# Fewer and wider attention matmuls, index scores between projections, and larger expert pieces in a two-block network kernel

## The chip, the cores and the metric

The kernel runs on one core of one Trainium2 chip. The metric is the device time of one execution in microseconds (us). The engines are PE (matrix products; PEld is its loading of weights), DVE, ACT and POOL (element-wise work) and SP (which issues DMAs here). Line numbers such as L1195 are those of the kernel before; in the changed kernel the same code stands a few to some fifty lines lower or higher.

## What is computed

Two network blocks run one after the other on 512 tokens of width 1024, all in fp32. The first block is a Hyena convolution and a differential attention (16 heads over 528 positions: the 512 tokens and 16 meta positions). The second has a sparse attention (DSA, 8 heads), a block attention (NSA, 8 heads) and a mixture of 32 experts. The parts that the change touches, cut from the reference:

```python
def attend(qb):                                   # differential attention, T = 528 keys
    s = jnp.einsum("bqhmd,bkhmd->bhmqk", qb, k) * scale
    p = jax.nn.softmax(s, axis=-1)
    p = p[:, :, 0] - lam * p[:, :, 1]
    return jnp.einsum("bhqk,bkhd->bqhd", p, v)

# DSA: index scores choose the keys (8 index heads of 32 columns)
idx_logit = jax.nn.relu(jnp.einsum('bthd,bsd->bths', qi, ki))
score = jnp.einsum('bth,bths->bts', wi, idx_logit)
_, sel = lax.top_k(where(causal, score, -inf), k_sel)
# ... softmax over the chosen keys, then p @ v with heads of 64 columns

# NSA: three branches per head (compressed, selected, window), 64 columns each
o = gc * o_cmp + gs * o_slc + gw * o_win

# MoE: two of 32 experts per token
gate, up = jnp.split(xb @ w_gate_up[e], 2, axis=-1)
y = (jax.nn.silu(gate) * up) @ w_down[e]
```

## The kernel before

The tokens stand in tiles of 128. A product that must be exact to fp32 is made of three matmuls of a number split in a high and a low part (`split`, L326 on ACT and L327 on DVE: `hi = cast(x)`, `lo = x - hi`): hi·hi, lo·hi and hi·lo. Where a plain fp32 operand is used (the experts), one matmul in the program is two records in the trace. A scheduler orders each engine's instructions from the order of the code, its priorities and the tiles that are free; generators that `yield` are merged by `interleave`, so that projections fill the time in which attention waits for its softmax.

*Differential attention* (about 830 to 1395 us) runs over eight groups of two heads. `v_proj` (L1195 to L1197) makes the values with the tokens as stationary operand, in five token tiles of 128, 128, 128, 128 and 16 rows (`TT`); the last one takes 3 x 8 matmuls for 16 rows. `S` (L1269, L1270) makes the scores, L1271 and L1272 the negative maximum and its scaling on DVE, L1274 the exponential. For each of the five key tiles the probabilities are transposed (L1291, into `pt`), split into `pth` and `ptl`, and multiplied with the values (L1296 `vh·pth`, L1297 `vh·ptl`, L1298 `vl·pth`); the fifth tile has 16 keys and takes three matmuls of its own per head.

*Projections and index scores of the second block* (about 1545 to 1697 us). The code makes the compressed keys, the queries and keys, the transposes of the compressed probabilities (`ptc`, L1570), then the index queries `qi`, and after all of that the index scores: for three token tiles `i` (256, 384 and 512 keys) and 8 heads, three matmuls of 32 rows each (L1585 to L1587) into one of two `pi` tiles, a ReLU on ACT (L1589) and a weighted sum on DVE (L1591, L1593).

*NSA and DSA attention* (1697 to 2005 us). `head` makes scores for two branches of a head (L1612 to L1614), the maximum (L1617) and its scaling by -0.125 (L1618), the exponential (L1621), then for each branch and each of four key tiles transposes (L1637), a split into `pth` and `ptl`, and three matmuls (L1644, L1646, L1647) into `po`. Keys are causal, so the four take 512, 384, 256 and 128 columns. The values stand in 128 columns of which 64 are zero (`vpad`), so that the two heads of a pair add up in one `po`. The gates' projections (L808 to L812 into `pg` and `S`) fill the waits.

*Mixture of experts* (2068 to 2406 us). After the router, `prepare(g)` makes the slot matrix `P` and the indices of the tokens of four experts (`cb`, L1922). For the first group `first_gather` picks the tokens with 64 matmuls (L1957) of the normed activations `Xh`, `Xl`; from the second group on an indirect DMA (L1931, issued on POOL) picks rows of `xd` into `xg`, and `turn` transposes them (L1971) and scales them into `Xs`. `gate_up` (L1988) and `down` (L2011) then use raw fp32 weights; two experts of 64 slots work side by side, one in the columns 0 to 63 of the PE array and one in 64 to 127 (`HALF`). `combine` (L2029) puts the results back.

The weights come in one stream of 1 MB pieces on SP's queue (`WeightStream`), into a ring of raw tiles: two at first, and from the end of the router's norm three more of `N_RAW` and four of the pool of split weights (L1833, L1834).

Of the kernel before, what the change touches and what calls it, by code (L numbers as in the profile page):

```python
# [10 lines left out]
FT = mybir.dt.float32  # L11
# [9 lines left out]
D = 1024  # L21
# [21 lines left out]
def host_consts():  # L43
# [109 lines left out]
    m[:, 193:201] = pi[:, None] + 128 * np.arange(8)[None, :]  # L153
# [37 lines left out]
class WeightStream:  # L191
# [156 lines left out]
N_RAW = 3  # L348
# [9 lines left out]
def weight_jobs(A):  # L358
# [29 lines left out]
    for m in range(KD):  # L388
# [24 lines left out]
    gu = A["w_gate_up_2"][0].rearrange("e (h a p) c -> e h p a c", p=128, h=2)  # L413
    dn = A["w_down_2"][0].rearrange("e (a p) c -> e p a c", p=128)
# [11 lines left out]
def build(tc, A, C, out):  # L426
# [3 lines left out]
    with ExitStack() as ctx:  # L430
# [52 lines left out]
        with tc.tile_pool(name="xn3", bufs=1, reuse_waits="tile") as xnp:  # L483
            k.xh = xnp.tile([128, KD, T], FR, name="xh")
            k.xl = xnp.tile([128, KD, T], FR, name="xl")
            pp = ppc.enter_context(tc.tile_pool(name="b2p", bufs=1, reuse_waits="tile", space=PSUM))
            with tc.tile_pool(name="hy3", bufs=1, reuse_waits="tile") as hp:
                yh = hp.tile([128, CT, T], FR, name="yh")
                yl0 = hp.tile([128, 2, T], FR, name="yl0")
                k.hT, k.yT = (hp.tile([128, KD, T], FT, name=n) for n in ("hT", "yT"))  # L490
                nc.gpsimd.dma_start(k.hT, k.hdram)
                yl = [yl0]
                for i, raw in enumerate(k.vx.tiles):
                    if i:
                        yl.append(k.xpool.tile([128, 2, T], FR, name="vx", bufs=CT // 2))
                    for c in range(2):
                        split(k, raw[:, c, 0:SEQ], yh[:, 2 * i + c, 0:SEQ], yl[i][:, c, 0:SEQ])
                yl = Pairs(yl)
                out_norm(k, yh, yl, (slice(META, PARTS_A.stop), PARTS_B), META, 3, 4, pp,
                         (("pj", 3), ("pm", 1), ("pi", 2)))  # L500
                nc.gpsimd.dma_start(k.hdram[:, :, META:], k.hT[:, :, META:])
            k.xctx.close()
# [1708 lines left out]
```

## Time and profile before

| | before |
|---|---|
| median of 3 runs | 2430.65 us (2430.28 to 2431.44) |
| the profiled execution | 2426.15 us, of which the span is 2424.1 us |
| PE busy | 2277.2 us, 94% of the span |
| PEld busy | 78% |
| DVE, ACT, POOL busy | 65%, 44%, 29% |
| DMA, mean | 126 GB/s |

The span is what the trace covers; the rest of an execution's time lies around it. PE is busy nearly all the time, so the span is a row of stages in which PE is either at work or waits for a short chain of another engine. The tables by stretch of time below are read stage by stage. A matmul's own duration overlaps the next one's, so what a matmul costs is the distance from its start to the next start.

### The profile page before, as it was taken

The numbers are of one execution on the slowest core, as the hardware profiler recorded it, in microseconds if no ns is written. First come the engines' busy times: TensorE is split into PE (matmuls) and PEld (weight loads), VectorE is DVE, ScalarE is ACT, GpSimd is POOL, SyncE is SP. The second block draws the span as 40 slices with busy tenths as digits, with TensorE's granted clock in tenths as the row PEclk, the third lists the DMA queues.
The fourth block names the chain that finished last, engine by engine and source line by source line (L and its number), as shares of the span: only waits on it lengthen the run. The fifth ranks groups of instructions, "written<-read, shape, count | busy, mean of one in ns | idle before, by whom it ended". The sixth has DMA issues, their size and how long they took to land. (4 is left out here: it accounts for less than half of the span.)

```text
span 2424.1 us, 38020 instructions
## 1 busy us (share of the span) xinstructions
PE 2277.2 (94%) x14644; PEld 1891.3 (78%) x14644; DVE 1574.4 (65%) x3065; ACT 1075.3 (44%) x2201; POOL 709.0 (29%) x713
## 2 busy tenths in 40 slices
PE   7999999998999989999999989888999999899997
PEld 6989999997889978888888879866777777544333
DVE  7777764438985696778778744587788764434333
ACT  5666654433344464656545544434444543211111
POOL 3454541115643242233232236332011112101000
PEclk9999999999999999999999999887999999899999
DMA  6333322222136421112111136621121324698983
GB/s 223 123 118 103 119 80 88 88 86 92 57 123 187 135 76 44 53 53 70 46 52 60 54 103 177 179 70 53 53 83 53 113 77 149 249 402 329 362 322 134
DMA packets 269329, 305.19 MB, mean 126 GB/s; under 512 B 20520, under 2 KB 212404, under 8 KB 268762
## 3 DMA queue, kind: packets, MB, share of 16 engines
q1 hardware_dynamic: 228048, 245.90, 30.8%
q10 hardware_dynamic: 35834, 32.64, 4.5%
q0 software_dynamic: 5264, 24.20, 2.6%
q8 instruction: 116, 1.90, 0.3%
q14 instruction: 67, 0.55, 0.1%
HBM read 277.13 MB, written 25.58 MB: 125 GB/s over the span
## 5 line engine op out<-in xcount | busy, mean ns | idle before, releaser
L261 DVE TENSOR_TENSOR wlo<-wraw,whi 128x1024 fp32r<-128x1024 f32 (+2 forms) x201 | 229.4, 1155 | 155.6 <-ACT whi L280 136.6
L261 POOL TENSOR_TENSOR wlo<-wraw,whi 128x1024 fp32r<-128x1024 f32 (+1 forms) x91 | 181.7, 2005 | 500.0 <-ACT whi L280 321.1
L280 ACT CAST whi<-wraw 128x1024 fp32r<-128x1024 f32 x198 | 206.1, 1047 | 181.9 <-PE pj L810 57.6
L808 PE MATMUL ps<-xh,whi 128*128 128x264 f32 x1024 | 215.0, 287 | 4.8 <-ACT hTd L581 4.5
L810 PE MATMUL ps<-xl,whi 128*128 128x264 f32 x1024 | 214.6, 287 | 0.0
L812 PE MATMUL ps<-xh,wlo 128*128 128x264 f32 x1024 | 212.2, 285 | 0.0
L808 PE MATMUL pj<-xh,whi 128*128 128x512 f32 (+2 forms) x544 | 191.0, 357 | 4.3 <-DVE rr L1180 2.9
L810 PE MATMUL pj<-xl,whi 128*128 128x512 f32 (+2 forms) x544 | 188.9, 353 | 0.0
L812 PE MATMUL pj<-xh,wlo 128*128 128x512 f32 (+2 forms) x544 | 188.4, 353 | 0.1
L808 PEld LDWEIGHTS ps<-xh,whi 128*128 128x128 f32 x1024 | 161.4, 190 | 7.0 <-ACT hTd L581 5.3
L810 PEld LDWEIGHTS ps<-xl,whi 128*128 128x128 f32 x1024 | 161.7, 189 | 1.8 <-issue 1.3
L812 PEld LDWEIGHTS ps<-xh,wlo 128*128 128x128 f32 x1024 | 161.4, 190 | 1.2 <-issue 0.8
L810 PE MATMUL pj<-vx,whi 128*128 128x256 f32 (+1 forms) x480 | 135.7, 284 | 0.6 <-DVE vx L327 0.6
L326 ACT CAST pth<-pt 128x512 fp32r<-128x512 f32 (+4 forms) x174 | 84.3, 497 | 113.3 <-PE pt L1637 62.1
L327 DVE TENSOR_TENSOR ptl<-pt,pth 128x512 fp32r<-128x512 f32 (+4 forms) x174 | 98.0, 573 | 50.9 <-ACT pth L326 50.5
L1274 ACT ACTIVATE p<-S,mx 128x528 f32<-128x528 f32 x128 | 89.6, 702 | 78.7 <-DVE mx L1272 58.4
L808 PEld LDWEIGHTS pj<-xh,whi 128*128 128x128 f32 x544 | 103.3, 192 | 19.0 <-DVE rr L1180 3.3
L812 PEld LDWEIGHTS pj<-xh,wlo 128*128 128x128 f32 x544 | 102.6, 192 | 14.1 <-issue 1.0
L810 PEld LDWEIGHTS pj<-xl,whi 128*128 128x128 f32 x544 | 102.9, 192 | 13.1 <-issue 1.0
L1271 DVE TENSOR_REDUCE mx<-S 128x1 f32<-128x528 f32 x128 | 88.7, 701 | 25.7 <-PE S L1270 25.4
L1988 PE MATMUL gu<-wraw,Xs 128*64 128x512 f32 x312 | 92.5, 600 | 0.0
L810 PEld LDWEIGHTS pj<-vx,whi 128*128 128x128 f32 x480 | 90.6, 189 | 1.0 <-DVE vx L327 1.0
(677 smaller groups left out, 6716.1 us busy)
## 6 DMA issues: line engine op xcount, KB each, us to landing
wraw<-in_w_gate_up_dram SPq DMA_DIRECT2D x39, 1024.0 KB
wraw<-in_hy_w_in_dram SPq DMA_DIRECT2D x32, 1024.0 KB
wraw<-in_da_w_in_dram SPq DMA_DIRECT2D x32, 1024.0 KB
wraw<-in_hy_w_out_dram SPq DMA_DIRECT2D x16, 1024.0 KB
wraw<-in_da_w_out_dram SPq DMA_DIRECT2D x16, 1024.0 KB
wraw<-in_w_down_dram SPq DMA_DIRECT2D x16, 1024.0 KB
whi<-in_w_gate_up_dram SPq DMA_DIRECT2D x25, 512.0 KB
wlo<-in_w_gate_up_dram SPq DMA_DIRECT2D x25, 512.0 KB
```

The lines of the kernel that those rows point to most:

```text
L261: eng.tensor_tensor(l, r, h.bitcast(FT), OP.subtract)
L280: nc.scalar.copy(hf, vf)
L326: nc.scalar.copy(hi, raw)
L327: (lo_eng or nc.vector).tensor_tensor(lo, raw, hi.bitcast(FT), OP.subtract)
L808: nc.tensor.matmul(ps[i], wh[:, kk, fsl], xh[:, kk, c], start=f, stop=False)
L810: nc.tensor.matmul(ps[i], wh[:, kk, fsl], xl[:, kk, c], start=False, stop=False)
L812: nc.tensor.matmul(ps[i], wl[:, kk, fsl], xh[:, kk, c], start=False, stop=l)
L1271: nc.vector.tensor_reduce(mx[:, m:m + 1], S[:, :, 0:TH], AX.XY, OP.max)
L1274: nc.scalar.activation(p.rearrange("p (a b) -> p a b", a=2), S[:, :, 0:TH], AF.Exp, bias=mx[:, m:m + 1], scale=0.125, accum_out=sm[:, m:m ...
L1988: nc.tensor.matmul(ps[o], xs[:, kk, o], w[:, a], start=(kk == 0), stop=(kk == 7))
```

## The change

1. Differential attention. The last 16 tokens of `v_proj` now take one stationary operand `xr` of 48 columns (high part, zeros, low part), so 16 matmuls instead of 24 per group; the fifth key tile's three products are one matmul with 80 rows (L1325 after), in which high and low parts of the probabilities (`pr`) and values (`vr`) stand in rows 0 to 15, 32 to 47 and 64 to 79. The scale 0.125 goes into the queries, and the maximum is negated as it is made, so L1272 (and L1618) are gone.
2. Second block. The index queries are projected first, and the index scores (`index_scores`) are merged with the rest of the projections (`rest`), two steps for each step of `rest`.
3. NSA and DSA. `pair` works on the two heads of a pair in place of the two branches of a head. Values and probabilities stay fp32: each key tile's probabilities are copied once (DVE for the first head, ACT for the second) and multiplied by one fp32 matmul of 64 columns per head, the heads in the two halves of the array. `vpad` and its splits are gone.
4. Mixture of experts. Expert weights are laid out so that a partition's piece is 8 KB for `wraw` (four consecutive rows of a matrix) in place of four of 2 KB; the activations are stored in a permuted order to fit (`xp_`), and the hidden values are transposed with a stride of 2. The first group is gathered by indirect DMA too; `first_gather` and `Xh`, `Xl` are gone. Six raw tiles instead of three are opened, before the output projection of the second block rather than after the router's norm. `yh`, `yl` and `PT` have 3 buffers instead of 4.

The core of the diff:

```diff
@@ WeightStream.more_raw, N_RAW, weight_jobs
     def more_raw(self, *pools):
+        i = self.nr % len(self.raw_at)
+        self.raw_at = self.raw_at[i:] + self.raw_at[:i]
         self.nr = len(self.raw_at)
-N_RAW = 3
+N_RAW = 6
+    job(w, 640, 256)
     for p in range(2):
         job(w, 936 + p * 256, 256, True)
...
-    job(w, 640, 256)
-    gu = A["w_gate_up_2"][0].rearrange("e (h a p) c -> e h p a c", p=128, h=2)
-    dn = A["w_down_2"][0].rearrange("e (a p) c -> e p a c", p=128)
+    gu = A["w_gate_up_2"][0].rearrange("e (h p a) c -> e h p a c", p=128, h=2)
+    dn = A["w_down_2"][0].rearrange("e (p a) c -> e p a c", p=128)
@@ differential attention
+                if i == 4:
+                    ps = ps[:48, 0:256]
+                    for kk in range(KD):
+                        nc.tensor.matmul(ps, xr[:, kk], wh[:, kk], start=(kk == 0), stop=False)
+                        nc.tensor.matmul(ps, xr[:, kk], wl[:, kk], start=False, stop=(kk == KD - 1))
...
-                        nc.vector.tensor_reduce(mx[:, m:m + 1], S[:, :, 0:TH], AX.XY, OP.max)
-                        nc.vector.tensor_scalar(mx[:, m:m + 1], mx[:, m:m + 1], -0.125, None, op0=OP.mult)
+                        nc.vector.tensor_reduce(mx[:, m:m + 1], S[:, :, 0:TH], AX.XY, OP.max, negate=True)
...
+                    if i == 4:
+                        r = pr_
+                        nc.scalar.copy(r[0:16], pt[:16])
+                        nc.scalar.copy(r[64:80], pt[:16])
+                        nc.vector.tensor_tensor(r[32:48], pt[:16], r[0:16].bitcast(FT), OP.subtract)
+                        nc.tensor.matmul(po, vrs[h % 3][0:80], r[0:80], start=False, stop=True)
+                        continue
@@ second block: projections and index scores
+            def index_scores():
+                for i in range(1, 4):
...
+                        yield
+            def rest():
...
+            interleave((rest(), 1), (index_scores(), 2))
@@ NSA and DSA: pair in place of head
-                    split(k, pt[:, c], th[:, c], tl[:, c])
...
-                    nc.tensor.matmul(po[:, c], vh[:, kt, vc], th[:, c], start=(first and b == 0 and kt == 0), stop=False,
...
-                    nc.tensor.matmul(po[:, c], vh[:, kt, vc], tl[:, c], start=False, stop=False, skip_group_check=True)
-                    nc.tensor.matmul(po[:, c], vl[:, kt, vc], th[:, c], start=False, stop=l, skip_group_check=True)
+                    t = wk.tile([128, 512], FT, name=f"pt{m}")
+                    (nc.scalar.copy if m else nc.vector.tensor_copy)(t[:, c], pt[:, c])
+                    th.append(t)
+                for o, t in zip(HALF, th):
+                    nc.tensor.matmul(po[o, c], v[:, kt], t[:, c], start=(first and kt == 0), stop=(last and kt == 3),
@@ mixture of experts
+    rawp = ctx.enter_context(tc.tile_pool(name="moew", bufs=1, reuse_waits="tile"))
+    k.W.more_raw((rawp, N_RAW))
...
-            split(k, tp, Xh[:, :, c], Xl[:, :, c])
...
-        k.W.more_raw((rawp, N_RAW), (k.W.hl_pool, 4))
+        k.W.more_raw((k.W.hl_pool, 4))
...
-                nc.tensor.transpose(tp[:, f], x[:, f * 128:f * 128 + 128], k.ident)
+                nc.tensor.transpose(tp[:, f], x[:, 256 * (f // 2) + f % 2:256 * (f // 2) + 256:2], k.ident)
...
-            yh, yl = (yp.tile([128, 2, 512], FR, name=n, bufs=4) for n in ("yh", "yl"))
+            yh, yl = (yp.tile([128, 2, 512], FR, name=n, bufs=3) for n in ("yh", "yl"))
...
-        first_gather()
+        prepare(0)
+        for _ in turn(0):
+            pass
```

Where the order of instructions changes, on PE. The index scores before: they begin after the last transposes of `ptc` (written to `pm`), and nothing else stands between them (`pi` is their result, `kih` and `kil` the index keys, `qih` and `qil` the index queries).

```order
L810 MATMUL pj<-xl,whi 128x512
L812 MATMUL pj<-xh,wlo 128x512
L1570 MATMUL pm<-ident,blk 128x128 x4
L1585 MATMUL pi<-kih,qih_19030 128x256
L1586 MATMUL pi<-kil,qih_19030 128x256
L1585 MATMUL pi<-kih,qih_19030 128x256
L1586 MATMUL pi<-kil,qih_19030 128x256
L1587 MATMUL pi<-kih,qil_19031 128x256 x2
L1585 MATMUL pi<-kih,qih_19030 128x256
```

After, on PE, the same work (now L1561 to L1563) at the first query projections of the second block (`scp` are the compressed scores, `pj` a projection):

```order
L1586 MATMUL scp<-kcl,rl 128x32
L1561 MATMUL pi<-kih,qih_18321 128x256
L1562 MATMUL pi<-kil,qih_18321 128x256
L1563 MATMUL pi<-kih,qil_18322 128x256
L1561 MATMUL pi<-kih,qih_18321 128x256
L1562 MATMUL pi<-kil,qih_18321 128x256
L1563 MATMUL pi<-kih,qil_18322 128x256
L813 MATMUL pj<-xl,whi 128x512
L815 MATMUL pj<-xh,wlo 128x512
```

Two heads' triples now stand between projections; 16 of the 24 triples do so, and the last eight, those with 512 keys, still follow one another after the last transposes.

In the NSA attention, PE before, the products of one branch (`vsh` and `vsl` are the split values, `pt<-ident` the transposes of the next branch):

```order
L1644 MATMUL po<-pth,vsh 128x512
L1646 MATMUL po<-ptl,vsh 128x512
L1647 MATMUL po<-pth,vsl 128x512
L1644 MATMUL po<-pth,vsh 128x384
L1637 MATMUL pt<-ident,P_19576 128x128
L1637 MATMUL pt<-ident,P_19593 128x128
L1646 MATMUL po<-ptl,vsh 128x384
L1647 MATMUL po<-pth,vsl 128x384
```

After, on PE at the same place (L1678 are the products of 64 columns, `w1k` is the buffer that the values took over, L1673 the transposes, L1648 to L1650 scores):

```order
L1648 MATMUL S<-ks0h,qs 128x512
L1649 MATMUL S<-ks0l,qs 128x512
L1650 LDWEIGHTS identb
L1650 MATMUL S<-causb,identb 128x128
L1673 MATMUL pt<-ident,P_19251 128x128
L1673 MATMUL pt<-ident,P_19311 128x128
L1678 MATMUL po<-pt_19343,w1k 64x384
L1678 MATMUL po<-pt_19350,w1k 64x256
L1673 MATMUL pt<-ident,P_19311 128x128
L1678 MATMUL po<-pt_19355,w1k 64x256
L1673 MATMUL pt<-ident,P_19311 128x128
```

The two heads' products stand side by side in part only. The 96 products form 76 runs with other PE work between them: 8 pairs of 512 columns, 7 of 128, 1 of 384, 1 of 256 and 3 of 384 beside 256, and 56 alone (8 of 512, 19 of 384, 19 of 256, 10 of 128).

At the start of the experts, PE before (`cb` are token indices, `rp` the router's counts); 64 matmuls of L1957 follow up to the first `gate_up`:

```order
L1905 MATMUL pg<-ident,rk 32x128 x4
L1922 MATMUL cb<-wr,P 128x8 x8
L1957 MATMUL ga<-P,xh 128x256
L1957 MATMUL ga<-P,xl 128x256
L1957 MATMUL ga<-P,xh 128x256
```

After, on PE at the same place:

```order
L1944 MATMUL pg<-ident,rk 32x128 x4
L1961 MATMUL cb<-wr,P 128x8 x16
L2041 LDWEIGHTS sel
L2041 MATMUL cb<-rkT,sel 128x512
L1994 MATMUL gu<-ident,xg 128x128 x8
L1961 MATMUL cb<-wr,P 128x8 x8
L1994 MATMUL ga<-ident,xg 128x128 x4
L2041 LDWEIGHTS sel
L2041 MATMUL cb<-rkT,sel 128x512
L2011 MATMUL gu<-wraw,Xs 64x512 x16
```

The 64 matmuls are gone; transposes of the gathered rows `xg` stand ahead of the first `gate_up` (L2011 after).

## Rows read from the trace of the kernel before

**Rows 1.** Stretches of time: us, busy (x instructions) by engine, PEclk, DMA share, GB/s

```profile
830.00:1395.00 565.00, 541.48 (x3550) 480.75 (x3550) 438.10 (x962) 318.13 (x673) 173.87 (x194) 0.97 0.19 58
...
1575.00:1670.00 95.00, 82.44 (x442) 70.44 (x442) 77.55 (x126) 36.79 (x68) 31.71 (x30) 0.89 0.24 67
1670.00:1697.00 27.00, 20.79 (x81) 14.18 (x79) 18.98 (x32) 12.53 (x27) 3.65 (x2) 0.58 0.15 40
1697.00:2005.00 308.00, 294.01 (x1495) 230.46 (x1494) 229.92 (x557) 136.64 (x359) 43.98 (x25) 0.98 0.24 77
...
2068.00:2097.00 29.00, 20.04 (x140) 17.53 (x140) 16.91 (x72) 7.31 (x19) 1.79 (x5) 0.76 0.69 254
2097.00:2406.00 309.00, 296.13 (x1250) 121.51 (x1247) 109.34 (x194) 53.74 (x104) 24.39 (x49) 1.00 0.86 321
```

**Rows 2.** Timeline of PE, differential attention: start us, duration us, instruction, count

```profile
1027.38 0.28 PE L1195 MATMUL pj<-whi,xh 128*16 128x256 f32 x1
1027.49 0.28 PE L1196 MATMUL pj<-wlo,xh 128*16 128x256 f32 x1
...
1061.59 0.49 PE L1297 MATMUL po<-ptl,vh 16*128 16x512 f32 x1
1061.93 0.39 PE L1298 MATMUL po<-pth,vl 16*128 16x512 f32 x1
```

**Rows 3.** Groups by line, 830 to 1395: busy us, mean ns, idle before

```profile
L1272 DVE TENSOR_SCALAR mx<-mx 128x1 f32<-128x1 f32 x128 | 17.8, 145 | 0.9
```

**Rows 4.** Waits of PE from 1575 to 1697: us in total, times, longest

```profile
PE pi L1585 <- ACT qih L326: 3.2, 1, 3.2
PE pi L1585 <- ACT rl L1589: 3.0, 10, 0.7
```

**Rows 5.** Timeline of PE, index scores with 512 keys

```profile
1689.48 1.28 PE L1585 MATMUL pi<-kih,qih 32*128 32x512 f32 x2 [0.30 <-ACT rl L1589]
...
1691.81 1.28 PE L1585 MATMUL pi<-kih,qih 32*128 32x512 f32 x2 [0.20 <-ACT rl L1589]
```

**Rows 6.** Timeline of PE, products of probabilities and values in NSA

```profile
1746.28 0.39 PE L1647 MATMUL po<-pth,vsl 128*128 128x512 f32 x1
1746.51 0.34 PE L1644 MATMUL po<-pth,vsh 128*128 128x384 f32 x1
...
1747.08 0.34 PE L1647 MATMUL po<-pth,vsl 128*128 128x384 f32 x1
1747.25 0.27 PE L1637 MATMUL pt<-ident,P 128*128 128x128 f32 x1
```

**Rows 7.** Waits of PE's weight loads from 1697 to 2005

```profile
PEld po L1646 <- DVE ptl L327: 6.9, 16, 1.1
...
PEld po L1644 <- ACT pth L326: 5.6, 12, 0.9
```

**Rows 8.** Groups by line, 1700 to 2000

```profile
L1618 DVE TENSOR_SCALAR mx<-mx 128x2 f32<-128x2 f32 x46 | 13.7, 299 | 0.2
```

**Rows 9.** Timeline of PE, expert matmuls: two side by side, then one alone

```profile
2160.11 0.59 PE L1988 MATMUL gu<-wraw,Xs 128*64 128x512 f32 x1
...
2160.97 0.59 PE L1988 MATMUL gu<-wraw,Xs 128*64 128x512 f32 x1
...
2163.11 1.02 PE L1988 MATMUL gu<-whi,Xs 128*64 128x512 f32 x2
2164.06 0.73 PE L2029 MATMUL cb<-yh,PT 128*128 128x512 f32 x2
```

**Rows 10.** Timeline of PE: the first of 64 gathering matmuls, and what follows them

```profile
2087.54 0.56 PE L1957 MATMUL ga<-P,xh 128*128 128x256 f32 x1
...
2096.66 1.08 PE L1988 MATMUL gu<-wraw,Xs 128*64 128x512 f32 x4
```

**Rows 11.** DMA issues, 2097 to 2380: count, median us from issue to landing

```profile
xg<-xd,ix POOLq DMA_INDIRECT x14, 7.9
```

**Rows 12.** Groups by line, 2097 to 2406: idle before the weight loads

```profile
L1988 PEld LDWEIGHTS gu<-wraw,Xs 128*64 128x64 f32 x308 | 24.9, 136 | 41.0 <-issue 38.6 <-DMA wlo<-in_w_gate_up_dram 0.7 <-DMA wraw<-in_w_gate_up_dram 0.5
```

More of the change, by code (lines that the diff above doesn't have):

```diff
@@ L482, in build @@
             ppc.close()
[L483 to L502, printed above, removed]
-            block2_mixer(k, A, C, out, pp, ppc)
@@ L506, in small_vectors @@
+        k.xctx.close()
+        block2_mixer(k, A, C, out, pp, ppc)
 def small_vectors(k, A, pp):
@@ L1417, in block2_mixer @@
         kal = sp.tile([128, 512], FR, name="kal")
-        ptc = {(g, x): kvp.tile([128, 512], FR, name=f"ptc{g}{x}") for g in range(2) for x in range(2)}
+        ptc = [kvp.tile([128, 512], FT, name=f"ptc{g}") for g in range(2)]
         KD2, qs = {}, {}
@@ L1567, in block2_mixer @@
-            for g in range(2):
-                pt = pp.tile([128, 4, 128], FT, name="pm", bufs=1)
-                for i in range(4):
-                    nc.tensor.transpose(pt[:, i], s2[:, i, 4 * g:4 * g + 4].rearrange("p h n -> p (h n)"), k.ident)
-                split(k, pt.rearrange("p a b -> p (a b)"), ptc[g, 0], ptc[g, 1])
             qi = []
@@ L1599, in block2_mixer, with pair @@
         pp = spc.enter_context(tc.tile_pool(name="b2ap", bufs=1, reuse_waits="tile", space=PSUM))
-        def head(po, br, first, last, cmp=None):
+        HALF = (slice(0, 64), slice(64, 128))
+        def pair(po, q, kk, v, mask, scale, first, last):
             P = []
@@ L1615, in head @@
+                w = mk.shape[1]
+                for m in range(2):
+                    o = S[:, m, 0:n]
+                    nc.tensor.matmul(o, q[m][:, qc], kk[0][:, 0:n], start=True, stop=False, skip_group_check=True)
+                    nc.tensor.matmul(o, q[m][:, qc], kk[1][:, 0:n], start=False, stop=False, skip_group_check=True)
+                    nc.tensor.matmul(S[:, m, n - w:n], identb, mk, start=False, stop=True, skip_group_check=True)
                 mx = wk.tile([128, 2], FT, name="mx")
@@ L1699, in tiles @@
             return [rp.tile([128, 1, 512], dt, name=name, bufs=bufs) for _ in range(n)]
-        oah, oal = (Pairs(tiles(4, "o", 8)) for _ in range(2))
+        opc = ctx.enter_context(ExitStack())
+        op = opc.enter_context(tc.tile_pool(name="b2o", bufs=1, reuse_waits="tile", side="right"))
+        oah, oal = (Pairs([op.tile([128, 1, 512], FR, name="o", bufs=8) for _ in range(4)]) for _ in range(2))
         obh, obl = (Pairs(tiles(4, "x", 16)) for _ in range(2))
@@ L1708, in mask @@
                 return maskadd[i] if i else causb
-            yield from head(po, [(qs[8 + 2 * p + m], m, (kah, kal), V["va"], mask, lambda i: None) for m in range(2)],
-                            True, True)
+            yield from pair(po, [qs[8 + 2 * p + m] for m in range(2)], (kah, kal), va, mask, None, True, True)
             split(k, po, oah[:, p], oal[:, p])
```

368 lines of the change are left out of this document (190 added, 178 removed).

## The prediction

> **What bounds the kernel now.** I read the table by stretches first: in each stretch, how much of it PE fills, and at what clock [rows 1]. The differential attention fills 541 of 565 us, the NSA and DSA attention 294 of 308, the experts 296 of 309 with a granted clock of 1.00. So three long stages are bound by PE, and an edit there is worth what it takes from PE's own row of starts, plus a little of the idle time. Two short stretches are different. From 1670 to 1697, the index scores, PE is granted only 0.58 of its clock, between the levels of 1.2 and 2.4 GHz, and DVE and ACT are half idle too: a chain sets the pace. From 2068 to 2097, the router and the first gather, DVE steps follow one another. Next I read the timelines of PE for prices, always from one start to the next, and last the waits of PE and of its weight loads, since a chain shows there.
>
> The sum is made against the profiled execution, 2426.15 us. The median of the runs is 2430.65, so 4.5 us are added at the end. Up to the differential attention the order of every engine's instructions is the same in both kernels, so nothing is counted there.
>
> **1. Differential attention: -20 us.** The last value tile goes from 24 to 16 matmuls in each of 8 groups. One of these costs 0.11 us from start to start [rows 2]; the loaded columns grow from 16 to 48, which the width of the moving side (256 in both) makes no dearer, so 64 x 0.11 = -7 us. The fifth key tile has three matmuls of 16 rows per head, and one costs 0.34 us [rows 2], though a full matmul of 512 columns costs 0.23 [rows 6]. One of 80 rows stays, and its price I take from the full one: 16 heads x (3 x 0.34 - 0.23) = -13 us. Its operand now needs two ACT copies and a DVE difference, one after another. In the order of the changed kernel at least 14 other PE instructions stand between the fifth tile's transposes and this matmul, and they hide the chain; without that cover it would be some 1.5 us for each of 16 heads, which would eat the gain, so the bound above is 0. On DVE 128 scalings of 145 ns go [rows 3]. They sit between a score and its exponential, but PE fills this stage, so I give 2 us for them and take these 2 off again for the small copies on ACT and POOL. Sum -20; bounds -26 (PE's idle 23 us also shrink a little) and -8.
>
> **2. Index scores: -14 us.** The stretch is 27 us [rows 1]. Two heads with 512 keys take 2.33 us from start to start, ended each time by the ReLU on ACT, which frees one of the two result tiles [rows 5]; at its start 3.2 us pass in waiting for the index query [rows 4]. In the changed kernel the last eight triples, of 512 keys, still stand alone: 4 x 2.33 = 9.3 us and 1 us to begin. The other 16 triples move between projections. At full clock they cost, with 0.17 us for 384 columns [rows 6] and half of 0.23 for 256, 8 x 3 x (0.17 + 0.115) = 6.8 us if they lengthen PE's row, and nothing if they fall into the 12.6 us that PE is idle from 1575 to 1670 [rows 1]. So the stretch costs 10.3 to 17.1 in place of 27: -10 to -17. I take -14, near the middle, since about half of that idle time is bound to single waits at fixed places. What is late next is DVE: it is busy 96.5 of these 122 us, so no more than 25 us can go. It loses the splits of the values there. Bounds -5 and -20.
>
> **3. NSA and DSA attention: -4 us, the least certain term.** PE's own work first. Before, a key tile takes three matmuls, at 0.23 us for 512 columns and 0.17 for 384 [rows 6], so by proportion 0.115 and 0.06 for 256 and 128: 24 sets x 3 x 0.575 = 41 us. After, one fp32 matmul of 64 columns per head. The experts show its price: two such side by side with 512 columns take 0.86 us (two records each) [rows 9]; one alone takes 0.95 until a matmul of full width starts [rows 9], so it is no cheaper alone than in a pair, and leaving the half width costs about 0.09. By the order the 96 products make 76 runs: 16 runs of 512 columns, 23 led by 384, 20 by 256 and 17 by 128, or 0.86 x (16 + 23 x 0.75 + 20 x 0.5 + 17 x 0.25) = 41 us, and with 0.09 on either side 76 x 0.18 = 14 us more. The compression's 24 products become 4 pairs: 24 x 0.23 against 4 x 0.86, -2. PE's row grows by 12 us. Had all heads been paired (48 runs, 0.86 x 30), it would have shrunk by 9 instead.
>
> Against that, waits go. The weight loads wait 12.5 us for `ptl` and `pth`, the two steps of the split [rows 7]; one copy is left, half on each engine. DVE also loses 46 scalings of 299 ns, 13.7 us, in the chain from score to exponential [rows 8]. I give -16 us for both: the 12.5, and a quarter of the 13.7. Sum -4. Bounds: -14 if the switching costs nothing and the rest holds; +12 if the fillers hid the waits already, so that only PE's row counts.
>
> What the profile shows is 0.09 us for a change of width. The Trainium skill, "TensorEngine Tiling (Array Packing)", section Key Properties, says that changing the tiling mode drains TensorE; it gives no price. The trace agrees that there is one. By the rule a drain comes with every one of the 76 runs; it is the fourth rival below.
>
> **4. First gather: 0 us.** The 64 matmuls from 2087.5 to 2096.7 go, -9.1 us [rows 10]. In their place: the indices to POOL, an indirect DMA, eight transposes and the scalings of the first pair. Such a DMA takes 7.9 us from issue to landing among the experts [rows 11], where the DMA share is 0.86; here, from 2068 to 2097, it is 0.69 [rows 1]. No row shows it on a quiet queue; I take 6. Transposes, scalings and the index copy come to some 3 us, and PE idles meanwhile. Sum 0; bounds -5 and +6.
>
> **5. Experts and output projection: -1 us.** The 8 KB pieces and the earlier, larger ring of raw tiles help only where PE waits for weights. The loads of `gate_up` wait 1.2 us for DMA in all [rows 12], so that is the gain. The transposes with a stride of 2 and three buffers instead of four for `yh` and `yl` can cost, and the first pairs' transposes now lie here; the runs of half width go from 72 to 77. Bounds -6 and +7. The output projection is bound by PE and loses an ACT and a DVE step beside it: nothing.
>
> **The sum.** -20 - 14 - 4 + 0 - 1 = -39, so 2387 for the profiled execution and **2391.6 us** for the median, 1.6% less.
>
> **Rivals.**
> *First*, the waits in the attention were hidden already. Then term 3 is +12 instead of -4, and the time 2408. For it: PE is idle only 14 of 308 us there [rows 1]. Against it: the 12.5 us of waiting weight loads, which a table of PE's busy time doesn't hold.
> *Second*, the index scores hand their wait on: the ReLU and the sums now stand in front of the rope steps of the projections on DVE and ACT, and PE waits for those. Term 2 is then -5 and the time 2401. DVE at 96.5 of 122 us speaks for it, half-idle ACT against.
> *Third*, the weights pace the experts after all, behind waits that the trace calls "issue" (38.6 us of the loads) [rows 12], and larger pieces free them. If 4% of the 309 us go, 12 us more, the time is 2380. A clock of 1.00 and 296 us of busy PE speak against it.
> *Fourth, slower than before*: each change of the array's width costs far more among the attention's short matmuls than the 0.09 us between the experts' long ones, because the array runs empty and the next weights load in the open. From 0.18 + 39/76 = 0.7 us per run the whole gain is gone; at 1.0 us the time is 2391.6 + 76 x 0.82 = 2454. The 0.95 us of the lone matmul [rows 9] speaks against it.
> *Fifth*, the terms cancel, with the chain of term 1 uncovered: about 2430.
>
> **How the numbers follow.** Forecast 0.56, first rival 0.16, second 0.09, third 0.07, fourth 0.07, fifth 0.05. About 0.2% is what a measurement of this kernel can tell from no change. Faster: 0.56 + 0.16 + 0.09 + 0.07 = 0.88; same 0.05; slower 0.07. The range leaves out the fourth and fifth rivals. Below it goes to 2366, which is terms 2, 3 and 4 near their better bounds together; above to 2418, the first rival with term 2 or 4 ten us worse.
>
> **What would show it.** In the changed trace the differential attention should be about 545 us long. The stretch of index scores alone after the last projection should be about 10 us, at a low clock still. The attention should be about 304 us, with runs of half width at 0.86 us per 512 columns and a tenth of a us at either end; the waits of the weight loads for the copy should be near zero. The first gather should show one DMA of 4 to 8 us with PE idle, and the experts still 309 us at a clock of 1.00. The prediction is wrong if the 80-row matmul waits for its operand, if the half-width matmuls cost clearly more than 0.95 us alone, or if a wait for DVE shows in front of the second block's projections.

## The result and the profile after

The changed kernel takes 2402.15 us (median of 5 runs, 2397.22 to 2414.01), the kernel before beside it 2430.28 (2425.81 to 2431.44). The ratio is 0.9892, with a 95% interval of 0.9868 to 0.9915: faster by 1.1%, 28 us. The forecast was 2391.6, with a range of 2366 to 2418. The profiled execution of the changed kernel took 2399.58 us, its span is 2397.8 us.

The page of the changed kernel, busy time by engine: PE is still busy for 94% of a span that is 26 us shorter.

```profile
PE 2258.6 (94%) x14396; PEld 1844.0 (77%) x14396; DVE 1536.0 (64%) x2845; ACT 1068.5 (45%) x2164; POOL 710.5 (30%) x709
```

To see where the 26.3 us of the two spans went, I cut both at the same instructions, by their starts on PE: the first value product of the differential attention, its last transposes (L1315), the first matmul of the compressed keys (L1471), the first NSA score (L1612), the last product of probabilities and values, the last sum of squares of the router's norm (L1806), the first `cb` (L1922), the first `gate_up` (L1988) and the last combining matmul (L2029).

| stretch, us | before | after | difference | forecast |
|---|---|---|---|---|
| up to the differential attention (unchanged code) | 846.6 | 848.8 | +2.2 | 0 |
| differential attention | 587.4 | 578.4 | -9.0 | -20 |
| its output projection | 151.4 | 152.2 | +0.8 | 0 |
| projections and index scores of block 2 | 110.8 | 94.2 | -16.6 | -14 |
| NSA and DSA attention | 292.5 | 283.1 | -9.4 | -4 |
| output projection and norm | 85.4 | 85.4 | 0.0 | 0 |
| router | 11.7 | 12.9 | +1.2 | 0 |
| first gather | 10.8 | 13.3 | +2.5 | 0 |
| experts | 315.4 | 316.6 | +1.2 | -1 |
| tail | 12.0 | 12.9 | +0.9 | 0 |

These are one execution of each. The unchanged code up to the differential attention took 846.6 to 856.6 us in the profiles of this study, and the differential attention of one and the same code 578.4 to 584.7 in seven of them, so a difference of 3 us or less in one row says little. In those seven PE is idle for 35 to 36 us each time; what differs is the granted clock of the stage, 0.979 where it took 578.4 us and 0.965 where it took 584.7. Before and after can be compared there: the clock is 0.981 and 0.979.

The stretches of the changed kernel, to be held against [rows 1] (us, busy by engine, PEclk, DMA share, GB/s): the differential attention, the two of block 2, the router with the gather, and the experts.

```profile
832.00:1385.00 553.00, 520.65 (x3451) 471.36 (x3452) 425.95 (x841) 330.49 (x693) 178.87 (x219) 0.97 0.19 59
...
1579.00:1674.00 95.00, 88.78 (x474) 71.97 (x475) 81.92 (x133) 44.38 (x81) 23.92 (x15) 0.86 0.24 67
1674.00:1957.00 283.00, 279.69 (x1330) 182.53 (x1329) 192.06 (x446) 114.95 (x304) 34.32 (x18) 0.99 0.23 75
...
2043.00:2068.00 25.00, 10.88 (x60) 9.07 (x60) 18.15 (x75) 3.02 (x10) 7.43 (x10) 0.53 0.35 128
2068.00:2385.00 317.00, 305.88 (x1259) 127.35 (x1258) 112.00 (x204) 58.76 (x113) 22.73 (x42) 0.97 0.78 305
```

Two things stand out. In the differential attention PE is idle for 32 us, where it was 23; PE's work fell by 21 us there and the stretch by less. In the NSA and DSA attention PE is idle for 3 us, where it was 14 in a longer window (13 in the 293 us from 1696 to 1989).

### The profile page after: what moved, and what is told of

The parts are those of the page before. It is cut to its first block, busy times and chain, and to the rows that moved or that the text cites. A ratio compares the mean times of both kernels' runs of the same rounds, so it can differ in the third digit from the quotient of the medians.

```text
span 2397.8 us, 37215 instructions
## 1 busy us (share of the span) xinstructions
PE 2258.6 (94%) x14396; PEld 1844.0 (77%) x14396; DVE 1536.0 (64%) x2845; ACT 1068.5 (45%) x2164; POOL 710.5 (30%) x709
## 5 line engine op out<-in xcount | busy, mean ns | idle before, releaser
L2011 PE MATMUL gu<-wraw,Xs 128*64 128x512 f32 x400 | 112.1, 626 | 0.0
L1300 DVE TENSOR_REDUCE mx<-S 128x1 f32<-128x528 f32 x128 | 88.9, 700 | 13.6 <-PE S L1299 12.2
L2055 DVE TENSOR_TENSOR acc<-acc,cb 128x512 f32<-128x512 f32 x64 | 43.1, 684 | 79.6 <-PE cb L2052 79.4
L1298 PE MATMUL S<-ks,qh 128*128 128x264 f32 x256 | 71.9, 301 | 11.9 <-ACT p L1302 11.7
```

The costliest lines, as they stand in the source:

```text
L1298: nc.tensor.matmul(S[:, i, 0:TH], qh[:, qs], ks[:, c], start=True, stop=False)
L1300: nc.vector.tensor_reduce(mx[:, m:m + 1], S[:, :, 0:TH], AX.XY, OP.max, negate=True)
L2011: nc.tensor.matmul(ps[o], xs[:, kk, o], w[:, a], start=(kk == 0), stop=(kk == 7))
```

## The experiments

**Part 1 alone.** The kernel before with the hunks of the differential attention only.

```diff
+                        nc.tensor.matmul(ps, xr[:, kk], wh[:, kk], start=(kk == 0), stop=False)
...
+                        nc.vector.tensor_reduce(mx[:, m:m + 1], S[:, :, 0:TH], AX.XY, OP.max, negate=True)
...
+                        nc.tensor.matmul(po, vrs[h % 3][0:80], r[0:80], start=False, stop=True)
```

> The kernel before with part 1 of the change alone (value tail, 80-row matmul, scale in the queries, negated maximum). In the changed kernel the stage from the first value product to the last transposes of the differential attention is 578.4 us against 587.4 before, 9.0 less, where 20 were forecast. Theory A (given back inside the stage: PE waits more for the exponentials): the stage is 575 to 581 us, everything later is as long as before, and the time is 8 to 12 us under the kernel before, about 2420. Rival B (the missing 11 us came from the other parts or from this one execution): the stage is about 567 us and the time about 2410.

Measured: 2421.18 us against 2430.05 beside it, a ratio of 0.9968 (0.9958 to 0.9978), some 8 us; the stage is 581.1 us. Theory A holds: the gain is cut inside the stage. The new matmuls themselves cost what was forecast. In the changed kernel's timeline of PE (start, duration) a 48-column matmul takes 0.12 us to the next start and the 80-row one 0.24:

```profile
874.01 0.28 PE L1207 MATMUL pt<-whi,xr 128*48 128x256 f32 x1
874.13 0.28 PE L1208 MATMUL pt<-wlo,xr 128*48 128x256 f32 x1
...
919.20 0.41 PE L1325 MATMUL po<-pr,vr 80*128 80x512 f32 x1
919.44 0.60 PE L1319 MATMUL pt<-ident,p 128*128 128x128 f32 x4
```

I summed over all matmul forms of the stage their count times the median distance to the next start: 542.7 us before, 522.3 in the changed kernel, 20.4 less. What stands above the medians, the waits, is 44.6 us before and 56.1 after. So 20 us of work went and 12 us of waits came. The waits of PE, us in total, times and longest, before (first three lines) and with part 1 alone (the rest):

```profile
PE S L1269 <- ACT p L1274: 5.4, 6, 2.3
PE pj L1195 <- DVE rr L1180: 3.5, 2, 2.3
PE pj L808 <- DVE rr L1180: 2.9, 2, 2.0
```

```profile
PE S L1295 <- ACT p L1299: 11.7, 8, 3.2
PE po L1220 <- DVE vl L327: 4.6, 1, 4.6
PE pj L808 <- DVE rr L1190: 4.6, 4, 2.1
PE po L1327 <- ACT pth L326: 3.7, 4, 2.1
```

A score waits for the exponential that frees its tile, 11.7 us in place of 5.4, and a product for ACT's cast of the probabilities (`pth`), 3.7 us where before there was none; the changed kernel has the same 11.7 and 3.7. The wait for the rope step (`rr`) did not grow, 4.6 us against 6.4, and the one for `vl` was 4.6 before too.

**More work for PE.** The value tail again with 24 matmuls per group.

```diff
-                        nc.tensor.matmul(ps, xr[:, kk], wh[:, kk], start=(kk == 0), stop=False)
-                        nc.tensor.matmul(ps, xr[:, kk], wl[:, kk], start=False, stop=(kk == KD - 1))
+                        nc.tensor.matmul(ps, k.xh[:, kk, 512:T], wh[:, kk], start=f, stop=False)
+                        nc.tensor.matmul(ps, k.xh[:, kk, 512:T], wl[:, kk], start=False, stop=False)
+                        nc.tensor.matmul(ps, k.xl[:, kk, 512:T], wh[:, kk], start=False, stop=l)
```

> The changed kernel with the value tail as before, 24 matmuls of 16 columns per group instead of 16 of 48: 64 matmuls of 0.118 us, 7.6 us more work for PE, the rest of the tail's steps on ACT, DVE and POOL alike. Theory A1 (where PE was freed, it now waits for other engines): the stage grows by at most 3 us, to 578 to 581. Rival A2 (PE sets the stage's length): it grows by 7 to 8 us, to 586.

Measured: 2405.48 us; the stage 581.5 us, 3 more, and together with the projection behind it 730.2 us against 730.6. The whole stage before, in the changed kernel and in this one, all three at a granted clock of 0.98:

```profile
846.60:1434.00 587.40, 561.84 (x3618) 492.79 (x3616) 439.23 (x952) 324.12 (x680) 185.98 (x204) 0.98 0.19 58
848.80:1427.20 578.40, 542.31 (x3522) 485.48 (x3520) 428.80 (x832) 338.20 (x704) 188.47 (x220) 0.98 0.20 59
856.60:1438.10 581.50, 549.77 (x3586) 489.70 (x3584) 430.38 (x832) 337.51 (x704) 183.89 (x220) 0.98 0.19 59
```

PE is busy 7.5 us longer than in the changed kernel, and its idle time falls from 36 to 32 us, so of 7.6 us of work about 3 show: theory A1. Most of the value tail's part of the gain was not there to be had. This is one profile, and the medians of the two kernels can't be told apart.

**Fewer copies on ACT.** Three of the new small copies moved to POOL and DVE.

```diff
-                        nc.scalar.copy(r[64:80], pt[:16])
+                        nc.gpsimd.tensor_copy(r[64:80], r[0:16])
-                    nc.scalar.copy(vlast, ps[32:48])
+                    nc.vector.tensor_copy(vlast, ps[32:48])
```

> The changed kernel with three of the small copies that part 1 added moved from ACT to POOL (rows 64 to 80 of pr, rows 0 to 16 of vr) and DVE (value tail out of PSUM). Theory A2b (the added ACT copies make the exponentials late): PE's wait of scores for the exponential falls from 11.7 us to about 5, as before, and the stage is 570 to 573 us. Rival A1 (the waits are those that more PE work hid before; which ACT copy stands there does not matter): wait and stage stay within 3 us of 11.7 and 578.4.

Measured: 2407.96 us; the stage 589.5 us, the longest of all, at a granted clock of 0.96, the lowest, so that its length is only in part the edit's. The wait for the exponential fell to 6.0 us, as A2b had it, but PE's idle time in the stage did not fall (38.8 us against 36.1): the wait for the rope step on DVE rose from 4.6 to 8.9 us (PE's waits in this kernel).

```profile
PE pj L811 <- DVE rr L1193: 8.9, 6, 2.8
PE S L1298 <- ACT p L1302: 6.0, 8, 2.4
```

A2b had the wait right and missed the stage, A1 missed both. Which engine makes the added copies decides which wait shows; moving them off ACT did not shorten the stage.

**Less work for ACT.** A copy of 32 half tiles by DMA in place of ACT.

```diff
-                    nc.scalar.copy(ql[b], ql[a])
+                    nc.sync.dma_start(ql[b].bitcast(FT), ql[a].bitcast(FT))
```

> The changed kernel with the second copy of each query's low part in the differential attention made by a DMA from SP's queue in place of ACT: 32 ACT copies of 0.62 us, 20 us of ACT's 330, are gone. The stage is 578 to 585 us long in six profiles of the same code. Theory K (ACT's queue, in which the exponential stands behind casts and copies, sets what PE waits for): the wait of scores for the exponential falls from 11.7 us to under 6 and the stage to 570 to 574. Rival L (the wait goes over to the next engine, as it went to DVE's rope steps when small copies went from ACT to POOL): one wait falls, another rises, and the stage stays at 577 us or more.

Measured: 2395.74 us; ACT's busy time in the stage fell from 330 to 308 us, the wait for the exponential only to 9.7, and the stage is 577.7 us. Rival L: 22 us of ACT's work buy nothing there. The median is some 6 us under the changed kernel, but the two profiled executions are 1.3 us apart, and the stretch that is clearly shorter, the projections of block 2 (89.3 us), was not edited, so I don't credit it.

**Two heads side by side.** One tile of two banks and one copy for both heads' transposed probabilities.

```diff
-                    pt = pp.tile([128, 512], FT, name="pt", bufs=2)
+                pt = pp.tile([128, 2, 512], FT, name="pt")
...
+                (nc.scalar.copy if kt % 2 else nc.vector.tensor_copy)(t2[:, :, c], pt[:, :, c])
```

> The changed kernel with both heads' transposed probabilities in one tile of two banks, copied by one instruction (DVE for even key tiles, ACT for odd), so that the two products of 64 columns follow one another: 47 runs of half width in place of 76, by the order. In the changed kernel the 192 records of these products take 52.4 us from start to start. Theory C (two halves side by side take the time of one): 0.86 x 30 + 47 x 0.18 = 34 us, and the attention stage falls from 283 to about 266 us, the time by some 15. Rival D (the one buffer of transposes brings the wait for the copy back, or halves side by side each pay): the stage is 278 us or more.

Measured: 2394.21 us, 0.986 (0.9836 to 0.9884); the attention 269.8 us in place of 283.1. Theory C, though 4 us short of what was expected in the stage, and 8 us in the median where 15 were. The 192 records of these products take 35.7 us from start to start, against 53.3 counted in the same way in the changed kernel. In the changed kernel one half alone costs as much as two, as its timeline shows: 384 columns of one head take 0.78 us to the next start, and 512 of both heads together 1.01.

```profile
1698.67 1.08 PE L1678 MATMUL po<-pt,w1k 128*64 128x512 f32 x4
1699.68 0.87 PE L1673 MATMUL pt<-ident,P 128*128 128x128 f32 x6
...
1701.88 0.86 PE L1678 MATMUL po<-pt,w1k 128*64 128x384 f32 x2
1702.66 0.50 PE L1648 MATMUL S<-kw0h,qs 128*128 128x512 f32 x1
```

Some of the 18 us came back as a wait here too: scores wait 8.3 us for the exponential (second line), where the changed kernel has 2.4 (first line).

```profile
PE S L1648 <- ACT P L1656: 2.4, 4, 0.9
```

```profile
PE S L1648 <- ACT P L1656: 8.3, 12, 1.1
```

**Index scores after the projections.**

```diff
-            interleave((rest(), 1), (index_scores(), 2))
+            for _ in rest():
+                pass
+            for _ in index_scores():
+                pass
```

> The changed kernel with the index scores after the rest of the projections again (all 60 of the last matmuls alone), the index queries still projected first. The stretch from the first matmul of the compressed keys to the first NSA score is 110.8 us before, 94.2 in the changed kernel. Theory E (the interleaving makes the gain): 103 to 108 us, the time 9 to 14 us above the changed kernel. Rival F (the earlier index queries and the values without splits make it): 94 to 98 us.

Measured: the stretch is 95.9 us. Theory E falls: without the interleaving the stretch is 1.7 us longer than in the profile of the changed kernel, 3 longer than the mean of the six profiles whose index code is that of the changed kernel and that were taken up to then (94.2, 94.5, 92.6, 91.9, 90.4, 94.0, mean 92.9; a later one has 89.3). The time, 2410.06 us, is 8 above, but 6 of that lie in the differential attention, where nothing was edited. Rival F, by its bounds: what is left of the change makes nearly all of the gain. Besides the earlier index queries and the values without splits, that is every other edit of the stretch (a buffer of its own for the ReLU, the compressed probabilities copied and not split). Where the time went, the stretches show. The first pair of lines is the changed kernel: projections with 16 triples merged in, then the end. The second pair has the projections alone, then all index scores. The single line behind is the kernel before, the same projections.

```profile
1596.00:1659.00 63.00, 63.00 (x367) 53.37 (x368) 54.25 (x87) 28.62 (x53) 16.83 (x12) 0.91 0.24 68
1659.00:1673.60 14.60, 11.59 (x36) 6.88 (x34) 11.91 (x18) 8.99 (x15) 3.10 (x1) 0.60 0.25 72
```

```profile
1606.00:1659.60 53.60, 52.72 (x323) 46.52 (x321) 47.09 (x75) 23.47 (x39) 17.18 (x12) 0.97 0.28 79
1659.60:1685.60 26.00, 22.86 (x81) 16.77 (x80) 18.29 (x31) 14.54 (x29) 2.35 (x1) 0.61 0.15 41
```

```profile
1602.00:1670.60 68.60, 61.09 (x330) 52.72 (x330) 52.62 (x91) 25.36 (x46) 17.89 (x16) 0.85 0.21 62
```

The merged triples shorten the end by 11.4 us, and lengthen the projections by 9.4: PE has no idle time left there to take them in, and the granted clock is 0.91 in place of 0.97. A projection matmul of 512 columns then takes 0.281 us from start to start on average, against 0.251. The lower clock does not come with the merging, though: the kernel with 2 KB pieces (first line) and the one with less work for ACT (second line) have the same merged code, and there the projections ran at 1.00, with 0.245 us per matmul.

```profile
1600.40:1659.60 59.20, 58.10 (x364) 49.38 (x362) 54.29 (x87) 28.48 (x53) 16.88 (x12) 1.00 0.26 72
1600.90:1659.00 58.10, 57.18 (x359) 48.63 (x357) 53.39 (x87) 28.49 (x53) 15.75 (x11) 1.00 0.27 73
```

So the merging lengthens PE's row by some 5 us at that clock and by 9 at 0.91, and it is worth 1.4 to 6.6 us (95.9 in the one profile without it, against 89.3 to 94.5). In the kernel before, the same projections had 7.5 us of idle PE and a clock of 0.85; without the merging, 0.9 us and 0.97.

**Three steps of index scores per step.**

```diff
-            interleave((rest(), 1), (index_scores(), 2))
+            interleave((rest(), 1), (index_scores(), 3))
```

> The changed kernel with three steps of the index scores for each step of the rest in place of two; by the order 6 triples stand alone at the end in place of 10. Theory E (what still stands alone costs 1.2 us per triple, as 2.33 us for two heads before): the stretch falls from 94.2 to about 90 us. Rival G (DVE, busy 82 of these 95 us, has become the bound): it stays within 2 us of 94.2.

Measured: 2399.18 us; the stretch 91.4 us, 2.8 less than in the profile of the changed kernel and 1.5 less than the mean. That is inside the scatter of the same code (89.3 to 94.5), and doesn't tell E and G apart.

**2 KB pieces again.**

```diff
-    gu = A["w_gate_up_2"][0].rearrange("e (h p a) c -> e h p a c", p=128, h=2)
+    gu = A["w_gate_up_2"][0].rearrange("e (h a p) c -> e h p a c", p=128, h=2)
-                nc.tensor.transpose(tp[:, f], x[:, 256 * (f // 2) + f % 2:256 * (f // 2) + 256:2], k.ident)
+                nc.tensor.transpose(tp[:, f], x[:, f * 128:f * 128 + 128], k.ident)
```

> The changed kernel with the expert weights in 2 KB pieces per partition as before, the activations in their plain order and the transposes of the hidden values without the stride of 2. The experts, from the first gate_up matmul to the last combining one, take 316.6 us in the changed kernel and 315.4 before. Theory H (PE sets the experts' length, the pieces do nothing for it): 315 to 317 us, and a lower DMA rate. Rival I (larger pieces help, and a dearer transpose eats it): the transposes become cheaper but PE waits for weights, 319 us or more.

Measured: 2397.23 us; the experts 313.5 us, against 314.6 to 316.7 in the seven profiles with 8 KB pieces taken up to then. Theory H as far as the weights go, though 313.5 lies below its bounds: PE doesn't wait for 2 KB pieces. The DMA rate fell by 3% only: 420 GB/s in an early stretch of the experts in the changed kernel (first line), 408 here (second line).

```profile
2090.00:2110.00 20.00, 20.00 (x97) 8.87 (x97) 7.73 (x14) 4.63 (x10) 0.95 (x1) 1.00 1.02 420
```

```profile
2085.00:2110.00 25.00, 25.00 (x121) 10.46 (x120) 9.00 (x17) 6.52 (x14) 0.95 (x1) 1.00 1.04 408
```

The strided transposes cost 9.4 us over the experts, the plain ones 8.6. The 8 KB layout brings nothing here and costs 1 to 3 us by this profile (later kernels with 2 KB pieces have 313.6 to 314.9).

**Three raw tiles, opened early.**

```diff
-N_RAW = 6
+N_RAW = 3
```

> The changed kernel with three raw weight tiles opened ahead of the output projection in place of six. Theory H (the ring is full before the experts begin, and PE sets their length): the experts 316 to 317 us, output projection and gather within 1 us. Rival J (the earlier prefetch pays, or costs): the experts 320 us or more, or the output projection's 41.8 us fall by 1 us or more.

Measured: 2418.16 us, 0.9956 (0.9939 to 0.9972); the output projection begins 9 us late (52.6 us from the last attention product to the first sum of squares, against 43.6), the experts take 316.7. Neither theory fits: the experts are as H had them, and the output projection grows, which J had falling. The timeline shows how. Between 1984.82 and 1987.1 SP issues 4 MB, three pieces of expert weights and one of the output projection. The second to fourth of the expert pieces are the first line (the last of them at 2000.88). ACT's loads of the router's weights (`wrt`) and its three loads of `h` are issued at the same time and right behind. The issue of the loads of `h` takes 8.94 us, and ACT's next cast stands behind it in ACT's queue. The load of `wrt` lands only at 2000.15; DVE scales it first, then makes `hn`, and this is what ends PE's wait of 12.2 us.

```profile
1985.92 15.29 SPq L232 DMA_DIRECT2D wraw<-in_w_gate_up_dram  x3
1986.51 0.82 ACTq L1828 DMA_DIRECT2D wrt<-in_w_expert_dram  x1
1987.37 8.94 ACTq L1854 DMA_DIRECT2D h<-hdram  x3
1996.35 1.99 ACT L282 CAST whi<-wraw 128x1024 fp32r<-128x1024 f32 x2 [9.65 <-issue]
...
2000.15 1.78 DVE L1830 TENSOR_SCALAR wrt<-wrt,vc 128x36 f32<-128x36 f32 x8 [1.49 <-DMA wrt<-in_w_expert_dram]
...
2003.54 1.11 PE L1845 MATMUL tp<-ident,hn 128*128 128x128 f32 x4 [12.23 <-DVE hn L1862]
```

In the changed kernel the router's weights are asked for 7 us earlier and land in under 3 us, and all but one of SP's expert pieces are issued behind the loads of `h`, which take 0.35 and 0.94 us to issue:

```profile
1979.19 0.59 ACTq L1828 DMA_DIRECT2D wrt<-in_w_expert_dram  x1
1982.00 3.43 DVE L1830 TENSOR_SCALAR wrt<-wrt,vc 128x36 f32<-128x36 f32 x8 [1.00 <-DMA wrt<-in_w_expert_dram]
...
1985.56 0.35 ACTq L1854 DMA_DIRECT2D h<-hdram  x1
1985.94 0.94 ACTq L1854 DMA_DIRECT2D h<-hdram  x2
1987.26 25.73 SPq L232 DMA_DIRECT2D wraw<-in_w_gate_up_dram  x7
```

The six tiles as such do nothing for the experts (316.6 and 316.7); opening them early put the weights beside these loads, and with six the order happens to fall well. That it is this order and not the size was read from the two timelines and not tried by itself.

**Combined.** Two-bank transposes, three index steps, 2 KB pieces, and the first gather's index copied first, its sums on DVE.

```diff
-            nc.gpsimd.tensor_tensor(s3, s8[:, :, 0:6:2], s8[:, :, 1:6:2], OP.add)
+            (nc.gpsimd if g else nc.vector).tensor_tensor(s3, s8[:, :, 0:6:2], s8[:, :, 1:6:2], OP.add)
```

> The changed kernel with the two-bank transposes of the attention, three steps of index scores per step of the rest, 2 KB expert pieces and plain transposes, and the index of the first gather copied first and its small sums for the first group on DVE, so that the indirect DMA starts earlier. If the single gains add up (13 in the attention, 1 to 3 in the index stretch, 1 to 3 in the experts, 1 to 2 in the gather): 2380 to 2388 us, 14 to 22 under the changed kernel. If the pieces and the index ratio were noise: 2387 to 2391.

Measured: 2390.57 us, 0.9838 (0.9815 to 0.9861): 40 us under the kernel before and 12 under the changed one, at the lower of the two outcomes. Attention 269.0 us, index stretch 91.4, experts 314.9, gather 13.0 against 13.3: the earlier index gave next to nothing.

**The merging of the differential attention.** The combined kernel with three, and with one and a half, steps of attention per step of projections.

```diff
-            interleave((chain(qk_proj(g + 1) if g < 7 else (), z_proj(Z_AFTER[g])), 1), (ahead(tc, attend(g), AHEAD), 2))
+            interleave((chain(qk_proj(g + 1) if g < 7 else (), z_proj(Z_AFTER[g])), 1), (ahead(tc, attend(g), AHEAD), 3))
```

> The combined kernel (label best, 2390.6 us, differential attention 578.4 us) with three steps of attention for each step of the next group's projections in place of two, so that a score stands earlier ahead of its use. Theory M (the order in which the stage's work is merged sets the 37 us of long gaps on PE): the stage changes by 4 us or more, shorter if the exponentials were late. Rival N (ACT, DVE and POOL steps form a chain that no merging shortens): 576 to 581 us.

> The combined kernel (label best) with one and a half steps of attention for each step of the next group's projections in place of two, the other direction: more projection work between one softmax step and the next. Theory M: the stage moves against the direction of three steps, by 4 us or more. Rival N: 576 to 581 us.

Measured: 2388.40 us (0.983, 0.9813 to 0.9846) with three, the stage 583.7 us; 2392.05 us with one and a half, the stage 588.1. The times agree with the combined kernel's. Both stages lie above N's bounds, and neither direction shortens the stage, so neither theory is borne out as put. With three steps PE is idle for 34 us of the stage, where the combined kernel has 36, and the granted clock is 0.966 in place of 0.979; with one and a half it is idle for 43 us. So the merging can lengthen the waits, but neither value shortens them by more than 2 us, and what sets the rest of them stays open. Three steps has the lowest median of this study, 42 us under the kernel before, though not clear of the combined kernel's.

## Why the prediction was right, and where it wasn't

The direction and the range held, and the size in part: 28 us against a forecast of 39. The step that failed is in term 1. Term 2 came out near its value by luck, for another reason than the one given, and in term 3 the price was right and the waits were undersized. Between the profiles the sum missed by 13 us: 11 in term 1, 5 in the stretches taken as unchanged, and 5 in terms 4 and 5, against 8 gained in terms 2 and 3.

**Term 1, -20 forecast, -9.0 measured (-6 with part 1 alone, at a lower clock).** The prices were right: 0.118 us for each value matmul, 0.24 for the 80-row one, and PE's own work fell by 20.4 us. The step that failed is the first sentence of the prediction's reading: a stretch in which PE is 96% busy was taken for one whose length is PE's row of starts. PE's 23 us of idle time were taken as what is left over. The runs show a second limit close behind, and the softmax chain over ACT, DVE and POOL is the likely one. Work of PE that stood between its steps was cover. With less of it PE's idle time grew from 26 to 36 us, where the bound of -26 had it shrink: 6 us of it for exponentials and 4 for the cast of the probabilities (part 1 alone). With a part of the work put back the stage grew by less than half of it (value tail), and when ACT was relieved, the wait went to DVE or stayed (fewer copies, less work for ACT). No single engine is the limit: DVE is busy 426 of 553 us and ACT 330. Which chain of steps it is, no run shows. The stated bound of -8 covers the measured value, the chosen one didn't; the bound of 0 that the term's own text gives for an uncovered operand chain was not needed, since the 80-row matmuls wait for their operand 0.6 us in all.

**Term 2, -14 forecast, -16.6 measured, by another mechanism.** The sum put the gain on 16 triples that move into idle time of the projections. Undone, that move costs 1.4 to 6.6 us. The idle time that was to take them in was gone already, and the triples lengthen PE's row, by 5 us at a clock of 1.00 (6.8 was the price given for that case). What removed the idle time, and with it the clock of 0.85, is in the other edits of the stretch, such as the earlier index queries, of which the sum counted the wait of 3.2 us at the start of the scores alone, and the values without splits, which it only names. Which of these matters was not tried. The second rival, a wait handed to DVE, did not show.

**Term 3, -4 forecast, -9.4 measured.** PE's row came out as worked out: 41 + 14 = 55 us forecast for the products, 53.3 measured. The first rival fell: PE's idle time went from 14 to 3 us. The waits and the shorter chain were worth some 5 us more than the 16 given: before, the 288 products took 64.3 us from start to start, 23 more than the 41 of their columns, where the sum had 12.5 for their operands. PE's waits longer than a few tenths of a microsecond are nearly gone. The 0.18 us per run that was worked out from [rows 9] is borne out: with 47 runs, 35.7 us less the 26 of the columns is 0.21 us per run, with 76 it is (53.3 - 41) / 76 = 0.16, small waits included. The fourth rival, 0.7 us and more, is out. The Trainium skill, "TensorEngine Tiling (Array Packing)", Key Properties, says that changing the tiling mode drains TensorE; the trace agrees that each change costs something, about 0.1 us.

**Term 4, 0 forecast, +2.5 measured.** The DMA was priced at 6 us and took less; the rest was late. In the changed kernel's timeline the index is ready at 2057.5, POOL first makes small sums and issues the DMA at 2058.83, the transposes start at 2063.36 and the first `gate_up` at 2068.27, since scalings on ACT and DVE and the next group's slot matrix on DVE alternate:

```profile
2057.48 1.18 POOL L1972 TENSOR_TENSOR s<-s 128x6 f32<-128x6 f32 x1 [12.64 <-DVE ix L1966]
2058.83 1.13 POOL L1969 DMA_INDIRECT xg<-xd,ix  x1 [0.17 <-DVE ovc L2115]
2063.36 1.97 PE L1994 MATMUL gu<-ident,xg 128*128 128x128 f32 x8 [2.25 <-DMA xg<-xd,ix]
2068.27 8.71 PE L2011 MATMUL gu<-wraw,Xs 128*64 128x512 f32 x32
```

The chain behind the landing, 4.9 us, was the undersized step (3 us for transposes, scalings and the index copy).

**Term 5, -1 forecast, +1.2 measured.** Right that the pieces and the ring bring nothing to the experts. The first `gate_up` now starts at the lower clock behind the idle gather: up to 2071.7 two records side by side take 0.85 us from start to start, and 0.43 behind it. Over the first 10 us the clock is 0.82, where it was 1.00; over the whole stretch it is 0.97, where it was 1.00. The third rival, weights that pace the experts, is out.

## What to carry to other kernels

A stage that is 96% busy on one engine can still be held by a chain of others just behind it. Before work taken from the busy engine is booked in full, ask what that work covered: the cheapest test is to put a part of it back and see whether the stage grows.

When a change moves work into idle time, look at whether another part of the same change has closed that idle time. And two half-width matmuls are worth their pairing only if they really stand side by side in the order; one copy that feeds both makes sure of it. Before the length of a stretch is put down to an edit, compare its granted clock: here one and the same code differed by 6 us that way.

## What the runs showed of the hardware

A half-width fp32 matmul of 512 columns alone costs as much PE time as two side by side (0.95 and 0.86 us), and each run of half-width matmuls takes some 0.16 to 0.21 us beyond its columns, the two changes of width included. The granted clock of one and the same code differs between executions: the projections with merged index scores ran at 0.91 (0.281 us per matmul of 512 columns) in one profile and at 1.00 (0.245 us) in two others; the short matmuls of 32 rows alone were granted 0.60. The issue of three loads on ACT's queue took 8.94 us when SP had issued 4 MB just ahead, 3.93 us in the kernel before and 1.3 us in the changed kernel, and ACT's own work waited behind it. Weight pieces of 2 KB per partition moved at 408 GB/s and of 8 KB at 420.
